# Top-k masks made beside the attention, and the memory's projections started with it, in a two-layer encoder on one core

## The chip, the cores and the metric

One Trainium2 chip, one NeuronCore of it. The time is device microseconds of one execution of the whole program. TensorE (PE in the rows, PEld its weight loads) multiplies, VectorE (DVE), ScalarE (ACT) and GpSimd (POOL) do elementwise work, SyncE (SP) issues the DMA transfers. Each engine takes its instructions in one fixed order and waits, at an instruction whose data are not there, with everything behind it. SBUF is the on-chip memory of 128 partitions, PSUM the eight banks into which TensorE writes. In the quoted rows sb is any SBUF buffer.

## The reference, cut to what matters

Two layers over x of 1024 tokens by 1024 features. The mixer of a layer has three branches: a gated convolution, DSA (each query attends to the 256 keys that a small indexer scores highest) and chunked band attention with a bias. Cross-attention into 256 memory tokens and a squared-ReLU MLP follow.

```python
def reference(x, mem, positions, w_in, ...):
    for l in range(DEPTH):                                   # DEPTH = 2
        mix = hybrid_mixer(x, positions, w_in[l], ...)
        x = layer_norm(ALPHA * x + mix, ...)
        cross = memory_cross_attention(x, mem, w_mq[l], w_mkv[l], w_mo[l])
        x = layer_norm(ALPHA * x + cross, ...)
        x = layer_norm(ALPHA * x + squared_relu_mlp(x, ...), ...)

def hybrid_mixer(...):
    proj = einsum(x, w_in)                # conv gates, dq dk dv, iq ik iw, cq ck cv
    y_conv = short_conv_mixer(...)
    y_dsa = dsa_attention(...)            # per query: top 256 of the indexer's scores,
                                          # softmax over them, times v; 6 heads of 64
    y_chk = chunk_band_attention(...)     # chunks of 64, band of 9 chunks; 6 heads of 64
    return einsum(concatenate([y_conv, y_dsa, y_chk]), w_out)

def memory_cross_attention(x, mem, w_q, w_kv, w_o):
    k, v = split(einsum(mem, w_kv), 2)    # these need no result of the mixer
    ...                                   # 4 heads of 256: softmax(q k) v, then w_o
```

## The kernel before, in words

**Arithmetic.** All of it is fp32, done on TensorE from two parts of each operand: a high part (a rounding cast) and a low part (what is left). A product is three matmuls, high x high (L340), low (L341, L342). An activation is split by a cast on ScalarE (L644) and a subtraction (L645, on VectorE or GpSimd). A weight is split when it is brought in: a load by SP's queue (L284), the high part's cast (L285), on ScalarE or, while `late` is set, on VectorE, and the low part on GpSimd (L286).

**What a layer does, in order.** First a front and a back run beside each other. The front computes the indexer's scores for query blocks 2 to 7 (128 queries each) and searches the 256th largest score of each query, bit by bit: 32 rounds in which blocks 7 and 6 are counted on ScalarE (L789) and blocks 5 to 2 on VectorE (L793). At the end of the search it makes for each of the six blocks a mask of 384 to 1024 columns, in 6 to 11 VectorE instructions (L845 to L860; the two large blocks also L828 to L843): it compares the scores with the threshold, counts what ties take, by a running sum (L856), and writes the mask (L860). The back computes the projections of the other branches, the convolution and its gate, and then the attention: the chunked one, 6 heads x 4 units of two query blocks, and the sparse one, 8 blocks x 2 groups of three heads.

**A unit of attention** multiplies scores into one of two banks for scores (L1054 chunked, L1184 sparse); VectorE adds bias or mask and takes the minimum, which empties the bank (L977); ScalarE takes the exponential (L983); GpSimd normalises (L994). Three units later in the pipeline TensorE transposes the rows (L1091, L1204), ScalarE and VectorE split them (L644, L645), and TensorE multiplies them with the values (L1105, L1213). Each head of the chunked part first prepares its queries (L1013 on VectorE, L1022 on GpSimd).

**The memory's projections** (`memory`) belong to the cross-attention, but need only the memory tokens: per layer 8 x 48 matmuls of 256 columns for keys and values, and 4 x 24 of 512 columns that multiply the values with the output weights. With them go 48 weights (32 of keys and values, 16 of the output), so 48 loads, casts and subtractions, and 16 blocks of products written to HBM (from L1373). They use one PSUM bank of their own, and serve as filler for TensorE beside the attention.

**What sets the order.** The pieces are Python generators that yield costs; `merge` always takes up the one whose sum of costs is least. `after(START, RATE, gen)` starts a generator at START and multiplies its costs by RATE. A scheduler then places the emitted instructions on each engine by priority and by its own model of durations; `shift` changes the priority of what a generator emits (FILL = 200 puts the memory's work back, 3000 the search). SBUF buffers come from one arena: a buffer that is freed is used again, and the new use waits for the old one.

Of the kernel before, what the change touches and what calls it, by code (L numbers as in the profile page):

```python
# [22 lines left out]
S = 1024  # L23
# [23 lines left out]
ROOMY = 8192  # L47
FILL = 200
TP = 2.5
START = 50  # L50
RATE = 2.0
EARLY = 0
STEP = 32
# [9 lines left out]
GROUPS = [(7, 6), (5, 4, 3, 2)]  # L63
# [192 lines left out]
class Weights:  # L256
# [17 lines left out]
    def _emit(self):  # L274
        k = self.k
        src, dims = self.specs[self.emitted]
        n = int(np.prod(dims))
        hl = k.sb.try_alloc(2 * n)
        if hl is None:
            return False  # L280
        st = self.stage[self.emitted % len(self.stage)].ap[:, :n]
        hi, lo = hl.r[:, :n], hl.r[:, n:]
        v = st if len(dims) == 1 else st.rearrange("p (a b) -> p a b", a=dims[0])
        k.nc.sync.dma_start(v, src)  # L284
        (k.nc.vector.tensor_copy if self.late else k.nc.scalar.copy)(hi, st)  # L285
        k.nc.gpsimd.tensor_tensor(lo, st, hi.bitcast(F32), op=ALU.subtract)  # L286
        self.units[self.emitted] = (hi, lo, hl)
        self.emitted += 1
        return True
# [21 lines left out]
class Kern:  # L311
# [449 lines left out]
    def topk(self, st):  # L761


        nc, sb = self.nc, self.sb


        groups = GROUPS
        junk, junk_a = sb.alloc(512), sb.alloc(512)
        tmp = [sb.alloc(S) for _ in range(2)]
        junkb = junk.ap.bitcast(BF16)  # L770
        junka = junk_a.ap.bitcast(BF16)
        col = sb.alloc(len(groups) * 32)
        state = []
# [7 lines left out]
        for bit in range(31, -1, -1):  # L781
            for g, blocks in enumerate(groups):
                cand, gone, cnt = state[g]
                ci, gi = cand.bitcast(I32), gone.bitcast(I32)
                for j, b in enumerate(blocks):
                    w = (b + 1) * P
                    x, c, n = st["score"][b].ap, cand[:, j : j + 1], cnt[:, j : j + 1]
# [26 lines left out]
                        op0=ALU.bitwise_xor, op1=ALU.bitwise_xor,  # L814
                    )
                yield TP * len(blocks) / 4
        for g, blocks in list(enumerate(groups))[::-1]:
            fl, cnt = state[g][0], state[g][2]
            for j, b in list(enumerate(blocks))[::-1]:
                w = (b + 1) * P  # L820
                sc = st["score"][b]
                tcol = fl[:, j : j + 1]
                eq, pre = (x.ap[:, :w] for x in tmp)
                if g == 0:


                    above, more = self.small(1), self.small(1)
                    nc.vector.tensor_scalar(  # L828
                        eq, sc.ap, tcol, None, op0=ALU.is_gt, op1=ALU.add,
                        accum_out=cnt[:, j : j + 1],  # L830
                    )
                    nc.vector.tensor_scalar(
                        eq, eq, -HIGH, HIGH, op0=ALU.mult, op1=ALU.add
                    )
                    nc.vector.tensor_tensor_reduce(
                        pre, sc.ap, eq, 1.0, HIGH, op0=ALU.add, op1=ALU.min,
                        accum_out=above,
                    )
                    nc.vector.tensor_scalar(
                        more.bitcast(I32), cnt[:, j : j + 1], float(TOPK), None,  # L840
                        op0=ALU.is_ge,
                    )
                    nc.vector.copy_predicated(tcol, more.bitcast(I32), above)  # L843

                nc.vector.tensor_scalar(  # L845
                    eq, sc.ap, tcol, BIG, op0=ALU.is_equal, op1=ALU.mult
                )
                nc.vector.tensor_scalar(
                    sc.ap, sc.ap, tcol, None, op0=ALU.is_le, op1=ALU.add,
                    accum_out=cnt[:, j : j + 1],  # L850
                )
                need = self.small(1)
                nc.vector.tensor_scalar(
                    need, cnt[:, j : j + 1], float(TOPK - w), BIG, op0=ALU.add, op1=ALU.mult
                )
                nc.vector.tensor_tensor_scan(pre, eq, eq, 0.0, op0=ALU.add, op1=ALU.max)  # L856
                nc.vector.scalar_tensor_tensor(
                    eq, pre, need, eq, op0=ALU.is_le, op1=ALU.mult
                )
                nc.vector.scalar_tensor_tensor(  # L860
                    sc.mask, sc.ap, BIG, eq, op0=ALU.mult, op1=ALU.subtract
                )
                sb.free(sc.high, self.w.late)
                yield 4.0
        for x in [junk, junk_a, col] + tmp:
            sb.free(x, self.w.late)

    def dsa_proj(self, l, xt, st):
        nc, sb = self.nc, self.sb
# [266 lines left out]
    def dsa_units(self, l, st):  # L1136


        nc, sb = self.nc, self.sb
# [33 lines left out]

        def scores(b, hg, heads):
            w = (b + 1) * P
            mask, qt = st["score"][b].mask, st["qt"][b]
            sm = self.small(3)
            for i in range(3):
# [763 lines left out]
    def build(self):  # L1942
        nc, sb = self.nc, self.sb
# [13 lines left out]
        for l in range(DEPTH):  # L1957
# [16 lines left out]
            def attention():  # L1974
                yield from self.pipeline(units())
                for x in ("dkT", "dv"):
                    sb.free(st.pop(x))

            def back():
                yield from self.dsa_proj(l, xt, st)  # L1980
                yield from self.chk_v(l, xt, st)
                for step in (
# [11 lines left out]
                self.ps.cls = dict(CLASSES)  # L1994
                self.w.reserve = RES
                self.w.late = LATE
                yield from self.merge(
                    attention(), self.after(START, RATE, self.shift(FILL, self.memory(l, st)))
                )

            self.ps.cls = {"S": (0, 1, 2, 3, 4, 5), "G": (6, 7)}
# [97 lines left out]
```

## Time and profile before

| what | value |
|---|---|
| median of the runs (three) | 3052.46 us (3051.95 to 3061.31) |
| profiled execution, its own time | 3054.18 us |
| its span | 3052.4 us |
| PE busy | 2894.9 us (95%), 14440 matmuls |
| DVE, ACT, POOL busy | 2239.0, 1527.2, 1317.6 us |
| mean granted TensorE clock | 0.973 |
| attention of layer 0, of layer 1 | about 284 to 580, 1809 to 2107 us of the span |

A row of a group reads: line, engine, operation, output and inputs with their shapes, how often; then busy time in us and the mean ns of one; then the idle time of that engine just ahead of these instructions and what ended it. A row of waits reads: waiting engine, buffer and line, the engine and line that it waits for, then us in all, how many, and the longest one. A row of time reads: start, duration, engine, line, operation.

### The profile page before, as it was taken

The page shows a single profiled execution, that of the slowest core. Times are in us where ns is not written, and L with a number is a line of the kernel's source. Part 1 is how long each engine was busy: PE and PEld are TensorE (multiplying, and loading weights), DVE is VectorE, ACT ScalarE, POOL GpSimd, SP SyncE. Part 2 cuts the span into 40 slices and gives each one's busy share as a digit, 9 for nine tenths or more (in the row PEclk, how much of TensorE's full clock was granted, in tenths as well). Part 3 has the DMA queues.
Part 4 walks back from the last instruction along what each step waited for, and adds up shares of the span by engine and source line. Part 5 has one row for each costly group of instructions (what it writes and reads, how often), then busy time and mean ns, then how long its engine had stood idle before and what let it go on. Part 6 is the DMA issues. An engine that isn't in the chain of part 4 may idle for free. (4 is left out here: it accounts for less than half of the span.)

```text
span 3052.4 us, 43458 instructions
## 1 busy us (share of the span) xinstructions
PE 2894.9 (95%) x14440; PEld 2452.0 (80%) x14440; DVE 2239.0 (73%) x4423; ACT 1527.2 (50%) x3074; POOL 1317.6 (43%) x1260
## 2 busy tenths in 40 slices
PE   8998799999999999999998987999999999999998
PEld 7886688878877788888787866887888777888886
DVE  5899978672478776777858998785725877667787
ACT  5676766513324455544456757665232344554442
POOL 4615566522335553232455154665223355532223
PEclk9999899999999999999999998999999999999999
DMA  3212133331325446755322121323312354466553
GB/s 125 55 43 57 50 102 113 116 114 39 105 101 175 165 154 223 247 186 189 123 71 55 39 65 41 116 93 125 114 52 101 110 174 162 152 249 227 182 180 115
DMA packets 261890, 374.14 MB, mean 123 GB/s; under 512 B 22560, under 2 KB 141344, under 8 KB 261664
## 3 DMA queue, kind: packets, MB, share of 16 engines
q1 hardware_dynamic: 261664, 371.35, 37.0%
q8 instruction: 114, 1.87, 0.2%
q14 instruction: 112, 0.92, 0.1%
HBM read 269.56 MB, written 95.42 MB: 120 GB/s over the span
## 5 line engine op out<-in xcount | busy, mean ns | idle before, releaser
L340 PE MATMUL banks<-sb,sb 128*128 128x512 f32 (+3 forms) x3776 | 1427.2, 379 | 31.8 <-DVE sb L645 11.7
L341 PE MATMUL banks<-sb,sb 128*128 128x512 f32 (+3 forms) x3776 | 1421.4, 377 | 6.0 <-POOL sb L286 5.9
L342 PE MATMUL banks<-sb,sb 128*128 128x512 f32 (+3 forms) x3776 | 1419.5, 377 | 6.5 <-POOL sb L645 6.5
L645 POOL TENSOR_TENSOR sb<-sb,sb 128x512 fp32r<-128x512 f32 (+1 forms) x428 | 588.1, 1386 | 946.1 <-ACT sb L644 834.9
L340 PEld LDWEIGHTS banks<-sb,sb 128*128 128x128 f32 x3776 | 717.0, 190 | 164.0 <-DVE sb L645 14.9
L342 PEld LDWEIGHTS banks<-sb,sb 128*128 128x128 f32 x3776 | 717.1, 190 | 132.0 <-POOL sb L645 7.3
L341 PEld LDWEIGHTS banks<-sb,sb 128*128 128x128 f32 x3776 | 717.6, 190 | 128.7 <-POOL sb L286 7.5
L644 ACT CAST sb<-sb 128x512 fp32r<-128x512 f32 (+1 forms) x788 | 452.5, 605 | 580.1 <-PE banks L341 135.1
L286 POOL TENSOR_TENSOR sb<-sb,sb 128x512 fp32r<-128x512 f32 (+2 forms) x288 | 376.3, 1319 | 512.0 <-ACT sb L285 403.7
L645 DVE TENSOR_TENSOR sb<-sb,sb 128x512 fp32r<-128x512 f32 x360 | 285.8, 821 | 41.6 <-ACT sb L644 41.3
L645 DVE TENSOR_TENSOR sb<-banks,sb 128x384 fp32r<-128x384 f32 (+2 forms) x324 | 187.8, 595 | 80.8 <-ACT sb L644 76.1
L644 ACT CAST sb<-banks 128x384 fp32r<-128x384 f32 (+2 forms) x324 | 160.0, 516 | 172.1 <-PE banks L1521 75.2
L793 DVE TENSOR_SCALAR_CACHE_REDUCE sb<-sb,sb 128x768 bf16<-128x768 f32 (+3 forms) x256 | 207.5, 811 | 4.9 <-POOL sb L749 2.3
L1685 DVE TENSOR_TENSOR sb<-sb,sb 128x512 f32<-128x512 f32 x160 | 158.4, 1025 | 56.9 <-ACT sb L1665 53.9
L1727 DVE TENSOR_TENSOR sb<-banks,sb 128x512 f32<-128x512 f32 x224 | 149.8, 683 | 45.9 <-PE banks L342 40.4
L983 ACT ACTIVATE sb<-sb,sb 128x640 f32<-128x640 f32 (+7 forms) x192 | 141.7, 739 | 77.5 <-DVE sb L977 73.2
L285 ACT CAST sb<-sb 128x512 fp32r<-128x512 f32 (+2 forms) x192 | 112.0, 599 | 125.9 <-PE banks L341 29.2
L994 POOL TENSOR_SCALAR sb<-sb,sb 128x128 f32<-128x128 f32 (+7 forms) x192 | 144.9, 770 | 66.6 <-DVE sb L992 60.6
L789 ACT ACTIVATE sb<-sb,sb 128x1024 bf16<-128x1024 f32 (+1 forms) x128 | 140.3, 1096 | 51.6 <-DVE sb L812 46.8
L1790 DVE TENSOR_TENSOR sb<-sb,sb 128x512 f32<-128x512 f32 x128 | 97.9, 767 | 70.5 <-DMA sb<-w_ff_dram 69.8
L1664 ACT ACTIVATE sb<-sb 128x512 f32<-128x512 f32 x128 | 80.7, 631 | 123.7 <-DVE sb L1727 123.5
L1582 DVE TENSOR_TENSOR sb<-sb,sb 128x512 f32<-128x512 f32 x96 | 91.6, 954 | 50.7 <-DMA h<-sb 30.7
(173 smaller groups left out, 3128.1 us busy)
## 6 DMA issues: line engine op xcount, KB each, us to landing
sb<-h SPq DMA_DIRECT2D x236, 256.0 KB, 3.1
h<-sb SPq DMA_DIRECT2D x224, 256.0 KB, 2.1
sb<-w_ff_dram SPq DMA_DIRECT2D x216, 256.0 KB, 3.1
sb<-w_ff_dram SPq DMA_DIRECT2D x64, 512.0 KB, 4.4
sb<-w_in_dram SPq DMA_DIRECT2D x64, 256.0 KB, 2.8
sb<-w_mkv_dram SPq DMA_DIRECT2D x64, 256.0 KB, 2.7
xs<-sb SPq DMA_DIRECT2D x24, 512.0 KB, 2.6
sb<-xs SPq DMA_DIRECT2D x24, 512.0 KB, 3.8
```

What stands on the lines that cost most here:

```text
L286: k.nc.gpsimd.tensor_tensor(lo, st, hi.bitcast(F32), op=ALU.subtract)
L340: mm(out, lh, rh, start=start, stop=False)
L341: mm(out, lh, rl, start=False, stop=False)
L342: mm(out, ll, rh, start=False, stop=stop)
L644: nc.scalar.copy(hi, src)
L645: eng.tensor_tensor(lo, src, hi.bitcast(F32), op=ALU.subtract)
L789: nc.scalar.activation(junka[:, :w], x, AF.Sign, bias=c, scale=-1.0, accum_out=n)
L793: nc.vector.tensor_scalar(junkb[:, :w], x, c, None, op0=ALU.is_ge, op1=ALU.add, accum_out=n)
L983: nc.scalar.activation(pt.ap, pt.ap, AF.Exp, bias=mn, scale=-1.0, accum_out=sm)
L994: nc.gpsimd.tensor_scalar(pt.ap, pt.ap, rc[:, i : i + 1], 0.0, op0=ALU.mult, op1=ALU.add)
L1685: nc.vector.tensor_tensor(z.ap, x, y, op=ALU.add if spec[1] == "+" else ALU.subtract)
L1727: nc.vector.tensor_tensor(r.ap, ps.ap, part[c, x].ap, op=ALU.add)
```

## The change

It has three parts. The masks are no longer made at the end of the search but by a generator of their own, `masks`, that runs beside the attention, a block per step; the scores of a sparse block run it on until the block's mask has been issued. Its two work buffers are taken per block, with the block's width, where the search held two of 1024 columns. The memory's projections start at cost 0 instead of 50 of the attention. And the high part of every weight is cast on ScalarE, while `late` is set too. What is computed, and with how many instructions, stays the same: only the 96 casts of the memory's weights (48 a layer) go from VectorE to ScalarE.

```diff
@@ -47,7 +47,7 @@
 ROOMY = 8192
 FILL = 200
 TP = 2.5
-START = 50
+START = 0
 RATE = 2.0
 EARLY = 0
 STEP = 32
@@ -282,7 +282,7 @@
         hi, lo = hl.r[:, :n], hl.r[:, n:]
         v = st if len(dims) == 1 else st.rearrange("p (a b) -> p a b", a=dims[0])
         k.nc.sync.dma_start(v, src)
-        (k.nc.vector.tensor_copy if self.late else k.nc.scalar.copy)(hi, st)
+        k.nc.scalar.copy(hi, st)
         k.nc.gpsimd.tensor_tensor(lo, st, hi.bitcast(F32), op=ALU.subtract)
         self.units[self.emitted] = (hi, lo, hl)
         self.emitted += 1
@@ -766,7 +766,6 @@
 
         groups = GROUPS
         junk, junk_a = sb.alloc(512), sb.alloc(512)
-        tmp = [sb.alloc(S) for _ in range(2)]
         junkb = junk.ap.bitcast(BF16)
         junka = junk_a.ap.bitcast(BF16)
         col = sb.alloc(len(groups) * 32)
@@ -814,13 +813,24 @@
                         op0=ALU.bitwise_xor, op1=ALU.bitwise_xor,
                     )
                 yield TP * len(blocks) / 4
-        for g, blocks in list(enumerate(groups))[::-1]:
+        sb.free(junk)
+        sb.free(junk_a)
+        st["found"] = state, col
+
+    def masks(self, st):
+
+        nc, sb = self.nc, self.sb
+        while "found" not in st:
+            yield 1.0
+        state, col = st.pop("found")
+        for g, blocks in list(enumerate(GROUPS))[::-1]:
             fl, cnt = state[g][0], state[g][2]
             for j, b in list(enumerate(blocks))[::-1]:
                 w = (b + 1) * P
                 sc = st["score"][b]
                 tcol = fl[:, j : j + 1]
-                eq, pre = (x.ap[:, :w] for x in tmp)
+                tmp = [sb.alloc(w) for _ in range(2)]
+                eq, pre = (x.ap for x in tmp)
                 if g == 0:
 
 
@@ -860,10 +870,11 @@
                 nc.vector.scalar_tensor_tensor(
                     sc.mask, sc.ap, BIG, eq, op0=ALU.mult, op1=ALU.subtract
                 )
-                sb.free(sc.high, self.w.late)
-                yield 4.0
-        for x in [junk, junk_a, col] + tmp:
-            sb.free(x, self.w.late)
+                for x in [sc.high] + tmp:
+                    sb.free(x, self.w.late)
+                st["masks"].add(b)
+                yield 7.5
+        sb.free(col, self.w.late)
 
     def dsa_proj(self, l, xt, st):
         nc, sb = self.nc, self.sb
@@ -1173,6 +1184,8 @@
 
         def scores(b, hg, heads):
             w = (b + 1) * P
+            while b not in st["masks"]:
+                next(st["mask steps"])
             mask, qt = st["score"][b].mask, st["qt"][b]
             sm = self.small(3)
             for i in range(3):
@@ -1994,8 +2007,16 @@
                 self.ps.cls = dict(CLASSES)
                 self.w.reserve = RES
                 self.w.late = LATE
+                st["masks"] = {0, 1}
+                st["mask steps"] = self.masks(st)
+
+                def mask_steps():
+                    for d in st["mask steps"]:
+                        yield 2.0 * d
+
                 yield from self.merge(
-                    attention(), self.after(START, RATE, self.shift(FILL, self.memory(l, st)))
+                    attention(), mask_steps(),
+                    self.after(START, RATE, self.shift(FILL, self.memory(l, st))),
                 )
 
             self.ps.cls = {"S": (0, 1, 2, 3, 4, 5), "G": (6, 7)}
```

What moves, at the three places that matter. The instructions of VectorE ahead of the first softmax step of layer 0, before (L856 to L860 are the mask of block 5, L828 and on the beginning of that of block 6, L1013 prepares a head's queries, L977 is the softmax step):

```order
L856 SCALAR_TENSOR_TENSOR sb_163<-sb_79 128x768
L1013 SCALAR_TENSOR_TENSOR sb_2723<-sb_1671,sb_2723 64x1024
L853 TENSOR_SCALAR sb_2510<-sb_1475 128x1
L857 SCALAR_TENSOR_TENSOR sb_79<-sb_163,sb_2510,sb_79 128x768
L860 SCALAR_TENSOR_TENSOR sb_281<-sb_280,sb_79 128x768
L828 TENSOR_SCALAR sb_79,sb_1475<-sb_282,sb_1475 128x896
L832 TENSOR_SCALAR sb_79<-sb_79 128x896
L839 TENSOR_SCALAR sb_2510<-sb_1475 128x1
L835 ISA sb_163,sb_2510<-sb_282,sb_79 128x896
L835 ISA sb_2510 128x1
L977 ISA sb_2706,sb_2510<-banks,sb_2628 128x128
```

and after (L799 and L811 are the search's last rounds, before L800 and L812; L954 is the convolution; L1024 was L1013, L988 was L977):

```order
L954 SCALAR_TENSOR_TENSOR sb_2512<-sb_149,sb_268,sb_2512 128x1022
L811 SCALAR_TENSOR_TENSOR sb_1475<-sb_1475 128x2
L799 TENSOR_SCALAR sb_1475<-sb_1475 128x1
L1024 SCALAR_TENSOR_TENSOR sb_2606<-sb_1671,sb_2606 64x1024
L799 TENSOR_SCALAR sb_1475<-sb_1475 128x1
L811 SCALAR_TENSOR_TENSOR sb_1475<-sb_1475 128x2
L1024 SCALAR_TENSOR_TENSOR sb_2774<-sb_1671,sb_2774 64x1024
L988 ISA sb_2657,sb_2654<-banks,sb_2604 128x128
L988 ISA sb_2654 128x1
L988 ISA sb_2762,sb_2654<-banks,sb_2604 128x256
```

Before, masks stand between the last of the search and the first softmax step; after, only the smallest one (384 columns) still does, some rows further up, and the others stand one instruction at a time between the softmax steps behind.

The same place on ScalarE, before (L983 is the exponential, L1021 prepares a head's keys):

```order
L983 ACT_TABLE_LOAD
L983 ACTIVATE sb_2706,sb_2510<-sb_2706,sb_2510 128x128
L983 ACTIVATE sb_2711,sb_2510<-sb_2711,sb_2510 128x256
L1021 CAST sb_2633<-sb_1937 64x512
L983 ACTIVATE sb_2716,sb_2510<-sb_2716,sb_2510 128x384
L983 ACTIVATE sb_2551,sb_2510<-sb_2551,sb_2510 128x512
L983 ACTIVATE sb_2743,sb_2510<-sb_2743,sb_2510 128x640
```

and after (L994 was L983; L285 is the cast of a weight's high part, L644 here that of the transposed memory tokens):

```order
L994 ACT_TABLE_LOAD
L994 ACTIVATE sb_2657,sb_2654<-sb_2657,sb_2654 128x128
L994 ACTIVATE sb_2762,sb_2654<-sb_2762,sb_2654 128x256
L285 CAST sb_2606<-sb_97 128x512
L994 ACTIVATE sb_2767,sb_2654<-sb_2767,sb_2654 128x384
L644 CAST sb_2667<-banks 128x4x128
L994 ACTIVATE sb_901,sb_2654<-sb_901,sb_2654 128x512
L285 CAST sb_2609<-sb_102 128x512
L994 ACTIVATE sb_930,sb_2654<-sb_930,sb_2654 128x640
```

The casts of the memory's weights now stand between the first exponentials.

TensorE in the sparse attention of the late blocks, before (L1184 scores, L1204 transposes, L1213 values; L340 to L342 are the memory's projections with the output weights):

```order
L1184 MATMUL banks<-sb_729,sb_4729 128x448 x2
L1213 MATMUL banks<-sb_3146,sb_620 128x384
L1204 MATMUL banks<-sb_67,sb_4690 128x128
L1204 MATMUL banks<-sb_67,sb_1082 128x128
L1204 MATMUL banks<-sb_67,sb_4757 128x128
L340 MATMUL banks<-sb_2658,sb_2674 128x512
L341 MATMUL banks<-sb_2658,sb_2674 128x512
L342 MATMUL banks<-sb_2658,sb_2674 128x512
L340 MATMUL banks<-sb_4838,sb_2674 128x512
L341 MATMUL banks<-sb_4838,sb_2674 128x512
L342 MATMUL banks<-sb_4838,sb_2674 128x512
```

and after (L1197, L1217 and L1226 are the same three lines):

```order
L1197 MATMUL banks<-sb_729,sb_4459 128x512 x4
L1226 MATMUL banks<-sb_5072,sb_620 128x384
L1217 MATMUL banks<-sb_67,sb_5052 128x128
L1217 MATMUL banks<-sb_67,sb_5079 128x128
L1217 MATMUL banks<-sb_67,sb_5101 128x128
L1226 MATMUL banks<-sb_5296,sb_620 128x384
L1226 MATMUL banks<-sb_4714,sb_620 128x384
L1226 MATMUL banks<-sb_4715,sb_620 128x384
L1226 MATMUL banks<-sb_2827,sb_620 128x384
```

Before, the memory's matmuls reach into the last blocks; after, all of them stand ahead of the values of sparse block 4, and the blocks behind it have none.

## The prediction

> **What bounds the kernel now.** I read the page first: which engine is nearly always busy, and where it is not.
>
> ```profile
> PE 2894.9 (95%) x14440; PEld 2452.0 (80%) x14440; DVE 2239.0 (73%) x4423; ACT 1527.2 (50%) x3074; POOL 1317.6 (43%) x1260
> ...
> PEclk9999899999999999999999998999999999999999
> ```
>
> TensorE works 95% of the span, so a microsecond is won only where PE idles or runs at a lower granted clock. Then the busy times by stretch, around the two attentions. The columns are: stretch, its length, busy us (and instructions) of PE, weight loads, DVE, ACT, POOL, then granted clock, DMA share, GB/s. The three rows of each layer are the attention's opening, its middle, and its tail (the sparse attention's blocks 4 to 7).
>
> ```profile
> 284.50:342.00 57.50, 31.40 (x130) 24.45 (x130) 53.27 (x99) 27.69 (x60) 41.76 (x32) 0.67 0.23 58
> 342.00:500.00 158.00, 146.93 (x1060) 134.12 (x1059) 130.30 (x375) 116.88 (x289) 97.38 (x124) 0.99 0.30 92
> 500.00:580.00 80.00, 74.86 (x470) 65.07 (x468) 61.32 (x146) 53.15 (x111) 46.90 (x41) 1.00 0.36 117
> 1809.00:1860.00 51.00, 28.88 (x109) 22.68 (x108) 48.54 (x98) 21.44 (x48) 34.56 (x33) 0.65 0.16 40
> 1860.00:2025.00 165.00, 152.40 (x1065) 138.37 (x1066) 131.63 (x379) 116.82 (x289) 104.40 (x127) 0.95 0.32 97
> 2025.00:2107.00 82.00, 80.91 (x513) 72.83 (x512) 62.16 (x146) 55.45 (x114) 37.42 (x35) 1.00 0.30 103
> ```
>
> The openings are holes: PE is busy 31.4 of 57.5 us, and at a clock of 0.67. At full clock that is 31.40 x 0.67 = 21.0 us of work; in layer 1, 28.88 x 0.65 = 18.8 us in 51.0. About 36 and 32 us are lost, while DVE is busy 93 to 95%. The waits of 284.5 to 342 say for whom PE waits, and DVE's order of time says what DVE does before its first softmax step (L977):
>
> ```profile
> PE banks L1054 <- DVE sb L977: 20.1, 3, 8.1
> PE banks L1054 <- DVE sb L1013: 4.7, 1, 4.7
> ...
> 283.37 1.69 DVE L857 SCALAR_TENSOR_TENSOR sb<-sb,sb,sb 128x640 f32<-128x640 f32 x1
> 304.45 0.28 DVE L977 CUSTOM_DVE_ANT_0 sb<-banks,sb 128x128 f32<-128x128 f32 x1
> ```
>
> The chunk scores (L1054) wait for banks that L977 empties, and L977 stands behind masks. The masks' main groups on DVE, 267 to 342:
>
> ```profile
> L856 DVE TENSOR_TENSOR_SCAN sb<-sb 128x384 f32<-128x384 f32 (+5 forms) x6 | 9.9, 1650 | 0.0
> L857 DVE SCALAR_TENSOR_TENSOR sb<-sb,sb,sb 128x384 f32<-128x384 f32 (+5 forms) x6 | 8.0, 1327 | 0.1
> L860 DVE SCALAR_TENSOR_TENSOR sb<-sb,sb 128x384 bf16<-128x384 f32 (+5 forms) x6 | 7.4, 1240 | 0.1
> L848 DVE TENSOR_SCALAR_CACHE_REDUCE sb<-sb,sb 128x384 f32<-128x384 f32 (+5 forms) x6 | 5.7, 946 | 0.1
> L845 DVE TENSOR_SCALAR sb<-sb,sb 128x384 f32<-128x384 f32 (+5 forms) x6 | 4.6, 767 | 0.1
> L835 DVE CUSTOM_DVE_ANT_0 sb<-sb,sb 128x896 f32<-128x896 f32 (+1 forms) x2 | 3.5, 1754 | 0.0
> ```
>
> These are 39.1 us a layer for six widths, 4224 columns together.
>
> **The change, part by part.** *The masks.* None is removed. In the new order the first one (384 columns, 9% of the work, 3.5 us) still stands in the search; about 36 us come later, single steps between softmax steps. The chunked attention does not need them, the sparse one does, block by block, and the last is done near the end of the chunked part: nobody waits for it early. What the opening keeps is the wait for L1013 (4.7 us) and a few us until the pipeline of units is filled, at half clock. I take 8 us, bounds 4.7 and 12.
>
> *The memory's projections from the start.* Each layer has 384 matmuls of 256 columns and 96 of 512 that need no attention. By the order all of them now stand before block 4 of the sparse attention. So they fill the opening and are missing in the tail. What they are worth in the tail of layer 0, by PE's groups in 500 to 580 (L340 to L342 are the memory's there):
>
> ```profile
> L1213 PE MATMUL banks<-sb,sb 128*128 128x384 f32 x99 | 29.5, 367 | 2.9 <-DVE sb L645 1.4 <-ACT sb L644 1.1
> L1204 PE MATMUL banks<-sb,sb 128*128 128x128 f32 x150 | 23.8, 272 | 0.0
> L1184 PE MATMUL banks<-sb,sb 128*128 128x448 f32 (+2 forms) x56 | 17.7, 395 | 1.0 <-DVE sb L977 1.0
> L340 PE MATMUL banks<-sb,sb 128*128 128x256 f32 (+1 forms) x51 | 17.1, 336 | 0.0
> L342 PE MATMUL banks<-sb,sb 128*128 128x256 f32 (+1 forms) x51 | 16.6, 325 | 0.0
> L341 PE MATMUL banks<-sb,sb 128*128 128x256 f32 (+1 forms) x51 | 16.2, 318 | 0.6 <-POOL sb L286 0.6
> ```
>
> The rows overlap each other; the memory's share is 49.9 of 120.9, and of PE's 74.86 us that is 30.9. They go to the front.
>
> *The high parts on ScalarE.* 48 casts a layer leave DVE. Their busy time by stretch (DVE, then ACT), the price of one on ACT, and how DVE waited for their loads:
>
> ```profile
> 284.50:500.00 215.50, 19.75 (x33) 1.22 (x2) 0.90 0.28 83
> 500.00:580.00 80.00, 9.41 (x16) 0.62 (x1) 1.00 0.36 117
> 2025.00:2107.00 82.00, 8.22 (x12) 0.00 (x0) 1.00 0.30 103
> ...
> L285 ACT CAST sb<-sb x192: 429/620/682, 4.8 to 2312.8; 128x512 fp32r<-128x512 f32 x160, 128x296 fp32r<-128x296 f32 x16, 128x384 fp32r<-128x384 f32 x16
>   DMA sb<-w_mkv_dram: 9.6, 13
> ...
> DMA to landing us min/median/max: 2.5/2.7/4.3
> ```
>
> DVE loses 29 us a layer; ACT gains 48 x 0.62 = 30. What the projections issue beside this moves with them: 48 loads and 16 writes of products a layer on SP's queue, a subtraction (L286) on POOL behind each cast. DMA engines are busy 0.23 to 0.36 of the attention, so I cost their earlier start at nothing; were that cover gone, rival 4 prices it.
>
> *The sum for layer 0.* Front work on PE: 21.0 + 146.93 x 0.99 + 30.9 = 197. At what rate? The middle has stretches without the memory's matmuls (342 to 380, 1860 to 1910) and with them:
>
> ```profile
> 342.00:380.00 38.00, 34.48 (x237) 29.50 (x236) 35.21 (x111) 36.47 (x87) 21.45 (x30) 1.00 0.27 66
> 380.00:500.00 120.00, 112.45 (x825) 104.61 (x824) 95.09 (x265) 80.42 (x203) 75.93 (x95) 0.99 0.31 100
> 1860.00:1910.00 50.00, 44.39 (x301) 38.62 (x301) 42.69 (x135) 43.87 (x106) 27.32 (x38) 0.94 0.19 52
> 1920.00:2025.00 105.00, 101.60 (x733) 94.66 (x733) 82.56 (x227) 66.81 (x167) 72.99 (x83) 0.97 0.38 119
> ```
>
> That is 78.9 of 88 us (0.90) without and 214.1 of 225 (0.95) with them. The new front is filled throughout, but it also carries the masks on DVE and the casts on ACT, so I take 0.93, bounds 0.90 and 0.95: 197 / 0.93 = 212 us. Do the others fit in? DVE: 53.3 + 130.3 - 19.8 plus some 7 us of masks that lay before 284.5 is 171; ACT: 27.7 + 116.9 + 46 x 0.62 plus 8 copies of the tail (0.59 each) is 178. Both are below 212.
>
> The tail, without filler: PE has 74.86 - 30.9 = 44 us left, DVE 61.32 - 9.41 = 51.9, ACT about 48. DVE is the longest. In the unfilled stretches above DVE was busy 77.9 of 88 us (0.89): 51.9 / 0.89 = 58 us, bounds 0.85 and 0.95 (61 and 55).
>
> Layer 0: 8 + 212 + 58 = 278 us against 295.5 (284.5 to 580), 17.5 less. Layer 1: front 18.8 + 152.40 x 0.95 + 30.9 = 194.5, over 0.93 is 209; tail (62.16 - 8.22) / 0.89 = 61; 8 + 209 + 61 = 278 against 298, 20 less. Together 37.5. The profiled execution took 3054.2 us, 1.7 above the median of the runs: 3054.2 - 37.5 - 1.7 = **3015 us**. Its own bounds: front 0.90 costs 14, 0.95 gives 9; the tail 5 or 8; the opening 8 or 7. Not all at once: 2998 to 3035.
>
> *A rule against it.* A mask step reads two SBUF operands, as L857 does, and POOL is at work all through the attention. L857 on 640 columns took 1.69 us (above) just ahead of a stretch in which POOL is busy 41.8 of 57.5 us, on 1024 columns only 1.28 while POOL stood idle 13.4 us:
>
> ```profile
> 328.81 1.28 DVE L857 SCALAR_TENSOR_TENSOR sb<-sb,sb,sb 128x1024 f32<-128x1024 f32 x1
> 334.23 1.28 POOL L1022 TENSOR_TENSOR sb<-sb,sb 64x512 fp32r<-64x512 f32 x1 [13.40 <-ACT sb L1021]
> ```
>
> The Trainium skill (SBUF — State Buffer, section SBUF: two separate sides) says that VectorE and GpSimd take a shared pair of ports as an exclusive lock for a whole instruction, the other blocked; the two rows agree. What it makes of the time is the third rival.
>
> **The rivals.**
>
> 1. *All of the hole is won.* Front at 0.95, tail at 0.95, opening 4.7: 4.7 + 207 + 55 = 267 and 4.7 + 205 + 57 = 267, so 28.5 + 31 less: 2993 us. For it: 0.97 in 1920 to 2025. Against: ACT and DVE are both above 80% then.
> 2. *The masks stall the softmax where they now stand.* Every step on DVE delays the L977 behind it, and two banks hold scores. If half of the 36 us shows on PE in each layer, 36 of the 37.5 us are gone: 3051, no change. Against: DVE has 41 us free in the front.
> 3. *POOL and masks exclude each other.* POOL in the front: 41.8 + 97.4 + 16 x 1.3 (its part of the moved units) = 160; with 36 of masks 196, under 212. So it decides nothing by itself; if the same 0.93 applied to a chain of 196 plus the three L1013 (2.1 us each in the hole), 203 / 0.93 = 218, six us a layer: 3027.
> 4. *Slower: ACT waits for the memory's loads.* A cast on ACT whose load is late holds every exponential (L983) and high part (L644) behind it. ACT has 34 us of slack a layer, and the gain is 19 more: 48 casts may wait 1.1 us each before the kernel loses. With half a landing time (1.35 us) each, ACT needs 178 + 65 = 243 us, 31 more than the front: 12 a layer lost, 3077 us. Against: DVE waited only 9.6 us for w_mkv in all, 0.15 us for each of the 64 loads. For: the loads are wanted twice as fast at the start.
> 5. *The change does not do what it says.* The order shows that it does, but for the first mask.
>
> **How the numbers follow.** A measurement of this kernel tells about 0.3%, 9 us, from no change. Chances: the forecast 0.54 and rival 3 0.09, both faster; a front near 0.88 with a slow tail, 3035 to 3043, 0.05, faster; rival 1 0.15, faster; rival 2 0.10, of it 0.08 within 0.3% and 0.02 slower; rival 4 0.07, slower. Together: faster 0.83, same 0.08, slower 0.09. The range 2989 to 3044 leaves out rival 4, most of rival 2 and a little of rival 1 below.
>
> **What would show it.** Right: the waits of PE L1054 (L1065 in the changed lines) for the softmax step fall from 20 us to a few in each layer; the granted clock of the openings rises from 0.67 and 0.65 to above 0.9; memory matmuls stand within 20 us of the first scores; the attention of layer 0 ends near 562 instead of 580; the tail runs with PE at about 0.75 to 0.8 and DVE at about 0.9. DVE's total falls by some 55 us, ACT's rises by some 60. Wrong: ACT idle before L285 for a DMA by tens of us (rival 4); L1065 still waiting for DVE in the whole chunked part (rival 2); longer POOL instructions there (rival 3); or a tail of over 65 us, where the lost filler takes back what the opening gave.

## The result, and the profile after

The changed kernel took 3025.95 us in the median (3022.03 to 3031.39, four runs); the kernel before, beside it, 3053.51 us. The ratio is 0.9906 (0.9882 to 0.9929): about 28 us faster. A later set, with more runs of the kernel before, gave 0.9909 (0.9892 to 0.9925). The forecast was 3015 us with a range of 2989 to 3044. The time lies in the range, but about a quarter of the forecast gain is missing.

The page of the changed kernel, the rows that answer to those shown of before:

```profile
PE 2892.3 (96%) x14440; PEld 2443.2 (81%) x14440; DVE 2169.2 (72%) x4327; ACT 1572.6 (52%) x3170; POOL 1310.0 (43%) x1260
...
PEclk9999999999999999999999999999999999999999
```

Both dips of the granted clock are gone. The same stretches of the two attentions, layer 1's moved by the 13 us by which its attention now begins earlier (first score at 1792.9 instead of 1805.8):

```profile
284.50:342.00 57.50, 50.23 (x308) 43.28 (x307) 35.15 (x97) 42.30 (x91) 42.26 (x43) 0.91 0.45 117
342.00:500.00 158.00, 141.80 (x963) 126.58 (x962) 128.04 (x329) 121.78 (x291) 110.75 (x122) 0.96 0.33 102
500.00:580.00 80.00, 74.35 (x425) 62.35 (x424) 64.14 (x166) 64.85 (x138) 31.91 (x34) 0.96 0.18 62
1796.00:1847.00 51.00, 43.07 (x283) 39.35 (x284) 37.09 (x101) 38.10 (x86) 38.80 (x38) 0.90 0.38 102
```

The openings hold 308 matmuls instead of 130, and 283 instead of 109. But the middle holds fewer than before, 963 instead of 1060, and its clock is 0.96 instead of 0.99. So some of what the opening won is given back behind it. The last value product of the attention comes 290.4 us after its first score in layer 0 (298.3 before), and 289.1 in layer 1 (301.5): 20.3 us of the profiled execution's 30. Another 7 us lie in the output projection and the cross-attention right behind, up to the first transposes of the MLP (L1521): from first score to there 565.5 and 564.7 us became 554.6 and 548.4. All the rest of the program gave 2.8 us.

TensorE's longest waits in the first opening, now:

```profile
PE banks L1336 <- DMA sb<-mem_dram: 3.0, 1, 3.0
PE banks L340 <- ACT sb L1386: 1.6, 1, 1.6
PE banks L1065 <- DVE sb L1024: 0.8, 1, 0.8
...
PE banks L1065 <- DVE sb L988: 0.4, 2, 0.2
```

The wait of the scores for the softmax step (20.1 us before) is down to 0.4; in layer 1's opening it fell from 12.1 to 3.9. There TensorE had also waited 9.2 us for GpSimd's normalisation (the longest 6.8, while GpSimd still had convolution steps and splits ahead of it); in the changed kernel's opening it is gone too. The new ones are short: the load of the memory tokens, and copies out of the memory's single bank.

### The profile page after: what moved, and what is told of

Its sections match the earlier page's. It is cut to its first block, busy times and chain, and to the rows that moved or that the text cites. A ratio compares the mean times of both kernels' runs of the same rounds, so it can differ in the third digit from the quotient of the medians.

```text
span 3022.4 us, 43528 instructions
## 1 busy us (share of the span) xinstructions
PE 2892.3 (96%) x14440; PEld 2443.2 (81%) x14440; DVE 2169.2 (72%) x4327; ACT 1572.6 (52%) x3170; POOL 1310.0 (43%) x1260
## 5 line engine op out<-in xcount | busy, mean ns | idle before, releaser
L340 PE MATMUL banks<-sb,sb 128*128 128x512 f32 (+3 forms) x3776 | 1425.9, 379 | 31.5 <-ACT sb L644 15.2
L342 PE MATMUL banks<-sb,sb 128*128 128x512 f32 (+3 forms) x3776 | 1414.9, 376 | 3.0 <-POOL sb L645 2.9
L645 POOL TENSOR_TENSOR sb<-sb,sb 128x512 fp32r<-128x512 f32 (+1 forms) x428 | 587.7, 1385 | 918.1 <-ACT sb L644 784.3
L340 PEld LDWEIGHTS banks<-sb,sb 128*128 128x128 f32 x3776 | 716.1, 190 | 164.1 <-ACT sb L644 17.4
L342 PEld LDWEIGHTS banks<-sb,sb 128*128 128x128 f32 x3776 | 714.8, 189 | 128.5 <-POOL sb L645 4.5
L644 ACT CAST sb<-sb 128x512 fp32r<-128x512 f32 (+1 forms) x788 | 452.3, 605 | 534.1 <-DVE sb L1595 96.7
L286 POOL TENSOR_TENSOR sb<-sb,sb 128x512 fp32r<-128x512 f32 (+2 forms) x288 | 386.1, 1357 | 490.2 <-ACT sb L285 448.3
L645 DVE TENSOR_TENSOR sb<-sb,sb 128x512 fp32r<-128x512 f32 x360 | 287.9, 827 | 44.6 <-ACT sb L644 43.8
L285 ACT CAST sb<-sb 128x512 fp32r<-128x512 f32 (+2 forms) x288 | 168.9, 605 | 153.8 <-PE banks L342 22.4
L644 ACT CAST sb<-banks 128x384 fp32r<-128x384 f32 (+2 forms) x324 | 158.6, 516 | 169.9 <-PE banks L1534 106.6
L645 DVE TENSOR_TENSOR sb<-banks,sb 128x384 fp32r<-128x384 f32 (+2 forms) x324 | 186.0, 594 | 76.6 <-ACT sb L644 74.2
L1698 DVE TENSOR_TENSOR sb<-sb,sb 128x512 f32<-128x512 f32 x160 | 155.5, 1005 | 65.6 <-ACT sb L1678 65.5
L994 ACT ACTIVATE sb<-sb,sb 128x640 f32<-128x640 f32 (+7 forms) x192 | 141.3, 738 | 29.4 <-DVE sb L988 24.3
L1803 DVE TENSOR_TENSOR sb<-sb,sb 128x512 f32<-128x512 f32 x128 | 98.6, 771 | 73.1 <-DMA sb<-w_ff_dram 73.0
L1595 DVE TENSOR_TENSOR sb<-sb,sb 128x512 f32<-128x512 f32 x96 | 85.6, 892 | 51.6 <-DMA h<-sb 28.8
```

The source lines that it names most:

```text
L285: k.nc.scalar.copy(hi, st)
L340: mm(out, lh, rh, start=start, stop=False)
L342: mm(out, ll, rh, start=False, stop=stop)
L644: nc.scalar.copy(hi, src)
L645: eng.tensor_tensor(lo, src, hi.bitcast(F32), op=ALU.subtract)
L994: nc.scalar.activation(pt.ap, pt.ap, AF.Exp, bias=mn, scale=-1.0, accum_out=sm)
```

## The experiments

All ratios are against the kernel before, run on the same chip beside the others; the sets ran on three chips, so kernels of different sets are compared by their ratios. Theory A, with the result known: VectorE paces the chunked part; what wins is that its masks no longer stand in one block ahead of the first softmax steps, and what is missing of the gain is what the masks cost where they stand now.

**One part at a time.** Four kernels take the change apart. The first has only the masks moved (START and the casts as before):

```diff
-START = 0
+START = 50
-        k.nc.scalar.copy(hi, st)
+        (k.nc.vector.tensor_copy if self.late else k.nc.scalar.copy)(hi, st)
```

> Only the masks move; the memory's projections start at 50 as before, their casts stay on VectorE. Theory A (VectorE sets the pace of the opening, and spreading the masks is what closes the hole): the 20 us waits of the chunk scores for the softmax step go, but the unfilled chunked part stays at VectorE's pace (about 119 us of its work in the 135 us up to the memory's start, 0.88; at 0.93 it takes 128), so 7 to 12 us a layer: 3030 to 3040 us. Rival B (the filler closes the hole, not the masks' move): within 5 us of before, 3048 to 3056 us.

The second keeps the early start and ScalarE's casts and runs all the mask steps at the search's end (it differs from the kernel before in the buffers, too: it has the change's smaller ones):

```diff
                 yield from self.shift(3000, self.topk(st))
+                st["masks"] = {0, 1}
+                st["mask steps"] = self.masks(st)
+                yield from self.shift(3000, st["mask steps"])
...
-                    attention(), mask_steps(),
+                    attention(),
```

> The masks stay at the search's end (with the new, smaller buffers), the memory starts at 0 with its casts on ScalarE. Theory A: the softmax steps still stand behind some 36 us of masks, PE can do only the memory matmuls that stand between the first scores, and the tail has lost its filler: 3040 to 3055 us. Rival B (filler is what counts): as good as the whole change, 3020 to 3032 us.

The third is the kernel before with `k.nc.scalar.copy(hi, st)` in L285 and nothing else:

> Only the high parts' casts go to ScalarE. They lie in the filled middle and in the tail, where PE is busy 93% and VectorE is not the bound. Theory A: within 0.3% of before, 3045 to 3057 us. Rival C (the casts on VectorE delay the memory's matmuls): 5 us or more a layer gained, under 3044 us. Rival D (ScalarE waits for loads): over 3060 us.

The fourth is the changed kernel with the casts back on VectorE:

> The whole change but for the casts, which stay on VectorE. Theory A (VectorE is the tightest engine of the front, where masks and casts now meet): the 30 us of casts a layer come back to it, and the front takes 5 to 10 us more a layer than with the whole change: 3033 to 3046 us. Rival D (the casts on ScalarE cost what they save): 3022 to 3031 us, as the whole change.

A fifth is the changed kernel with START = 50:

> The whole change but for the early start: the memory's projections begin at 50 again. Masks alone gave a ratio of 0.9920, the casts alone 0.9978, the whole change 0.9906. Theory A (the early start carries filler from the tail to the front and is worth nothing in sum): the two add up, 0.988 to 0.991. Rival B (part of the gain needs the filler in the opening): 0.992 or more.

And the change itself was measured once more:

> The changed kernel itself once more, beside more runs of the kernel before, since the other kernels are compared with its ratio of 0.9906 (0.9882 to 0.9929). Theory A (the early start is worth nothing or costs a little, for masks and casts without it gave 0.9892): 0.989 to 0.992. Rival B (the early start does win): under 0.989.

| masks moved | start at 0 | casts on ScalarE | ratio (95% interval) |
|---|---|---|---|
| no | no | yes | 0.9978 (0.9968 to 0.9987) |
| no | yes | yes | 0.9980 (0.9969 to 0.9991) |
| yes | no | no | 0.9920 (0.9903 to 0.9937) |
| yes | yes | no | 0.9928 (0.9913 to 0.9942) |
| yes | no | yes | 0.9892 (0.9876 to 0.9908) |
| yes | yes | yes | 0.9909 (0.9892 to 0.9925) |

Read in pairs. The masks' move is worth 0.0080 alone, 0.0086 beside ScalarE's casts, 0.0071 beside these and the early start: 22 to 26 us of 3055, so nearly the whole gain. In the third pair both kernels have the small buffers, so the gain does not come from these. ScalarE's casts are worth 0.0022, 0.0028 and 0.0019 (the last within the noise of its two ratios): 6 to 9 us for some 60 us of work taken off VectorE. The early start is worth nothing in any pair: +0.0002, +0.0008, +0.0017, each within the intervals. Theory A held in the first, third and fifth run. In the fourth the casts back on VectorE cost 6 us where I had priced 5 to 10 a layer, so by its ratio that kernel ended between the two theories (its 3037.1 us lie in theory A's range only because the kernel before took 3058 us on that chip). In the second the sum is theory A's, but the layers are not: in its profiled execution (3046.1 us, one of its fastest) layer 0 became 12.5 us shorter than before from first score to L1521 (553.0) and layer 1 11.5 us longer (576.2). Its waits show what stays when the masks do not move:

```profile
PE banks L1065 <- DVE sb L988: 18.7, 10, 12.3
...
PE banks L1065 <- DVE sb L988: 15.5, 10, 9.2
```

The first row is layer 0, the second layer 1. The scores still wait for the softmax step, and the attention from the first score to the last value product took 301.5 and 302.1 us, no less than before (298.3 and 301.5). So the filler made up for nothing there. The layers differ behind the attention, up to L1521: 251.5 us with 1259 matmuls in layer 0, 274.1 us with 1328 in layer 1 (before 267.2 with 1299, and 263.2 with 1292). In layer 0 more matmuls had already been placed among the attention's last; what put them there is not settled.

**Why the early start is worth nothing.** Here are the chunked part (first to last chunk score) and the sparse part (first to last value product) of both layers, of the changed kernel:

```profile
286.80:438.00 151.20, 131.59 (x856) 115.75 (x857) 118.56 (x295) 109.86 (x243) 112.48 (x109) 0.94 0.41 115
459.60:577.20 117.60, 110.89 (x679) 95.40 (x678) 91.38 (x244) 95.43 (x213) 51.79 (x60) 0.96 0.20 66
1792.90:1938.10 145.20, 123.12 (x834) 110.30 (x832) 116.14 (x293) 107.09 (x240) 107.78 (x105) 0.95 0.39 110
1962.70:2082.00 119.30, 113.15 (x692) 96.06 (x693) 92.79 (x237) 93.60 (x208) 57.50 (x64) 0.99 0.21 71
```

and of the kernel with masks and casts but without the early start:

```profile
286.90:410.00 123.10, 102.53 (x629) 88.31 (x630) 103.91 (x284) 92.89 (x212) 76.97 (x88) 0.89 0.25 67
430.40:573.00 142.60, 136.24 (x898) 120.40 (x897) 96.72 (x249) 109.39 (x242) 79.88 (x82) 1.00 0.32 102
1795.20:1914.60 119.40, 95.94 (x618) 82.09 (x617) 100.85 (x281) 88.65 (x207) 74.11 (x88) 0.94 0.25 72
1939.50:2075.90 136.40, 130.47 (x856) 116.85 (x854) 95.02 (x239) 107.24 (x234) 77.91 (x80) 0.99 0.33 109
```

The early start puts 227 more matmuls into layer 0's chunked part, which takes 28.1 us longer: 0.124 us for each. It takes 219 out of the sparse part, which takes 25.0 us less: 0.114 each. Layer 1 reads the same way, 216 more in 25.8 us, and 164 fewer in 17.1. That is near what a matmul costs where TensorE never idles (20.00 us busy for 157 of them in 480 to 500 of the kernel before, 0.127 each). These 157 have other widths, so by width: of those moved into layer 0's chunked part some 199 have 256 columns and 48 have 512, and back to back these start every 0.12 and 0.23 us, so together some 33 us; 28.1 is most of it. The unfilled chunked part showed PE busy 102.5 of 123.1 us, and still the filler did not go into the 20 idle us: with it 19.6 are idle. The row alone does not say why; the engines of a unit wait for each other in turn, and a filler matmul ahead of a score in TensorE's order makes that score late. What is shown is the price, not this reason. The whole layer gives the same answer: with the early start the attention is 4.3 and 8.4 us longer (290.4 and 289.1 us against 286.1 and 280.7) and holds 12 and 34 more matmuls; the stretch behind it, up to L1521, has as many fewer and is 6.3 and 10.8 us shorter.

**What the masks cost where they now stand.** The changed kernel without the running sum and the step behind it:

```diff
-                nc.vector.tensor_tensor_scan(pre, eq, eq, 0.0, op0=ALU.add, op1=ALU.max)
-                nc.vector.scalar_tensor_tensor(
-                    eq, pre, need, eq, op0=ALU.is_le, op1=ALU.mult
-                )
```

> The whole change, but the masks leave out the handling of ties (the running sum and the step behind it), so about 18 of the 36 us of mask work a layer are not done. Theory A (the masks, now between the softmax steps, slow the front through VectorE): 4 to 9 us a layer faster than the whole change, ratio 0.985 to 0.988. Rival E (VectorE has room there, as the prediction's sum has it): within 2 us a layer of the whole change, 0.9895 to 0.9915.

It took a ratio of 0.9833 (0.9817 to 0.9849), more than theory A had asked for: 0.0076 below the changed kernel, 23 us or 11.6 a layer, for some 18 us of VectorE's work a layer (0.6 us for each; by the two intervals 0.4 to 0.8). The parts that shrank (chunked, sparse, by layer):

```profile
291.50:431.90 140.40, 122.44 (x834) 110.08 (x833) 100.79 (x281) 106.93 (x240) 104.98 (x109) 0.94 0.42 120
455.60:568.90 113.30, 105.58 (x670) 90.94 (x669) 88.56 (x237) 94.03 (x208) 51.08 (x60) 1.00 0.20 64
1783.50:1921.20 137.70, 121.79 (x833) 109.62 (x833) 102.26 (x282) 105.02 (x235) 98.78 (x103) 0.95 0.40 115
```

The chunked part, in which the masks stand, is 10.8 and 7.5 us shorter; the sparse part of layer 0 4.3. So VectorE, busy only 118.6 of 151.2 us in the changed kernel's chunked part, has no free room for these steps: a microsecond of them costs about 0.6. Whether the other half of the mask work costs as much was not tried. One place where this is seen, 400 to 440 of the changed kernel, and the same stretch before:

```profile
400.00:420.00 20.00, 18.27 (x117) 16.36 (x118) 19.62 (x45) 12.87 (x29) 12.90 (x10) 0.91 0.52 160
420.00:440.00 20.00, 16.71 (x117) 14.32 (x115) 19.18 (x45) 12.99 (x32) 14.91 (x16) 0.99 0.28 85
```

```profile
400.00:420.00 20.00, 19.17 (x162) 19.15 (x163) 14.18 (x39) 8.73 (x21) 17.20 (x18) 1.00 0.35 107
420.00:440.00 20.00, 19.89 (x150) 18.59 (x150) 14.14 (x50) 16.74 (x50) 11.37 (x18) 1.00 0.38 126
```

VectorE is busy 38.8 of 40 us there, with the masks of the two large blocks, and TensorE gets 234 matmuls through instead of 312. The two stretches do not hold the same work, so this is an example and no measure of the masks' cost.

**Moving the masks about.** Three times as far apart (the costs of `mask_steps` times 6 instead of 2), then this with RATE = 3:

> The whole change, with the masks' steps three times as far apart (costs times 6 instead of 2): they are done after 45, 84, 108, 113 and 120 of a layer's 144 softmax steps instead of 23, 35, 40, 57 and 64. Theory A (VectorE is over 95% busy in 400 to 440 because masks crowd there): 2 to 6 us a layer faster than the whole change, ratio 0.986 to 0.989. Rival E: no difference, 0.990 to 0.992.

> As with the masks spread, and the memory's projections at rate 3 instead of 2, from 0 as in the change: by the order their matmuls now reach block 6 of the sparse attention, so neither the opening nor the tail is without filler. Theory A (the tail pays for what the front was given, since without filler its PE waits for the splits): 3 to 8 us a layer faster than with the masks spread alone, ratio 0.982 to 0.986. Rival F (the filler is worth the same wherever it stands): as with the masks spread alone, within 0.001.

0.9946 (0.9931 to 0.9962) and 0.9920 (0.9904 to 0.9935). The first went against both theories: it is 11 us slower than the change. Its chunked and sparse part of layer 0:

```profile
288.90:425.40 136.50, 126.05 (x850) 113.72 (x851) 87.22 (x257) 107.56 (x241) 97.68 (x108) 0.94 0.43 119
448.70:587.70 139.00, 118.10 (x663) 94.83 (x661) 114.05 (x282) 93.95 (x208) 56.61 (x62) 0.91 0.18 59
```

The chunked part is indeed 14.7 us shorter than the changed kernel's. But the masks of the large blocks now stand in the sparse part, whose late blocks have no filler: VectorE's busy time there goes from 91.4 to 114.1 us, and the part takes 139.0 us instead of 117.6. RATE = 3 wins 0.0026 on that, 8 us or 4 a layer, as theory A had it, though from a worse kernel than the change; the intervals leave this gain just clear of noise.

> The whole change with the memory's projections at rate 3 instead of 2 and the masks' steps at 1.5 instead of 2 (with 2 the buffers do not fit): the masks are done at nearly the same softmax steps (63 of 144 instead of 64), the memory's matmuls stand in the order from the first head to sparse block 6. Theory A (filler is worth the same in the front as in the tail as long as both are short of it, so that spreading wins a little): 0.986 to 0.989. Rival F (worth the same wherever it stands): 0.9895 to 0.9915.

> As with the masks moved and the casts on ScalarE, memory from 50 (ratio 0.9892), and the masks' steps half as far apart: done after 5, 23, 33, 43 and 51 softmax steps of a layer instead of 25, 33, 53, 65 and 84. Masks three times as far apart had cost 0.004. Theory A (masks belong where the softmax steps need VectorE least; late ones meet the sparse part, which needs it most): 0.986 to 0.989. Rival H (early masks crowd the opening again, and the chunk scores wait): 0.991 or more.

Rate 3 with the masks nearly where they were (the costs of their steps times 1.5): 0.9933 (0.9920 to 0.9947), 7 us slower than the change; neither theory had that. Masks half as far apart, without the early start: 0.9955 (0.9942 to 0.9967), 19 us slower than the same kernel with the change's spacing; rival H was right. The chunked part of layer 0 in that last kernel:

```profile
288.00:418.30 130.30, 100.38 (x596) 87.31 (x597) 112.93 (x297) 91.48 (x209) 77.47 (x85) 0.86 0.21 57
```

and its longest waits of layer 0's attention:

```profile
PE banks L1065 <- DVE sb L988: 11.0, 7, 6.1
PE banks L1102 <- POOL sb L1005: 8.3, 6, 2.3
```

The chunk scores wait for the softmax step again (11.0 us, 7.0 with the change's spacing), and the chunked part takes 130.3 us instead of 123.1. The longest wait, 6.1 us, is not only a matter of crowding: right ahead of it VectorE stood still for 3.6 us at a mask step (L855), until a convolution step on GpSimd (L970) was done. So the spacing of the change lies between two losses: earlier masks hold up the opening, later ones the sparse part. Why rate 3 alone loses is not settled; its chunked parts take 147.0 and 158.3 us.

**Another engine for a part of the masks.** The last step on GpSimd:

```diff
-                nc.vector.scalar_tensor_tensor(
-                    sc.mask, sc.ap, BIG, eq, op0=ALU.mult, op1=ALU.subtract
-                )
+                nc.gpsimd.tensor_scalar(
+                    pre, sc.ap, BIG, 0.0, op0=ALU.mult, op1=ALU.add
+                )
+                nc.gpsimd.tensor_tensor(sc.mask, pre, eq, op=ALU.subtract)
```

> The whole change, with the last step of every mask on GpSimd as two instructions instead of one on VectorE: some 7 us of VectorE's 36 us of mask work a layer go, GpSimd gets some 20 us. Leaving out 18 us a layer had given 0.0073 against the whole change (0.9833 against 0.9906), 0.6 us for each us. Theory A (VectorE's time between the softmax steps is what the masks cost): 4 us a layer faster than the whole change, ratio 0.987 to 0.9895. Rival G (GpSimd, 70% busy in the chunked part, becomes late with the normalisation and the low parts): 0.991 or more.

0.9911 (0.9897 to 0.9924), no difference to the change. It is rival G's outcome; GpSimd's busy time in layer 0's chunked part rose from 112.5 to 121.9 us, and VectorE's fell by 3.2, less than half of the 7.1 us that the step had taken in that layer. That GpSimd's lateness ate the gain is not shown; nor is what made VectorE's other work there longer.

## Why the prediction was right, and where its sum was off

**The bound.** Right. The holes at the openings were the masks' doing: moving them alone gives a ratio of 0.9920, and PE's wait of 20.1 us for the softmax step in layer 0's opening is down to 2.1 in that kernel.

**The sum.** To read it by its own steps I cut the attention near where the prediction did, at the 40th value product of the sparse part (the count at 500 and 2025 before; at 511 and 2016.5 of the changed kernel it is 38, and the 40th starts at 513.1 and 2017.0, so the fronts are short by 2.1 and 0.5 us and the tails long by as much). The columns are those of the stretches above:

```profile
284.50:511.00 226.50, 203.04 (x1336) 179.94 (x1335) 170.90 (x450) 171.99 (x398) 156.33 (x169) 0.95 0.37 108
511.00:573.00 62.00, 56.35 (x332) 46.60 (x331) 51.45 (x133) 53.62 (x115) 26.20 (x26) 0.97 0.08 29
1796.00:2016.50 220.50, 194.96 (x1305) 173.35 (x1306) 168.46 (x453) 166.65 (x390) 147.00 (x162) 0.95 0.36 107
2016.50:2082.00 65.50, 61.55 (x357) 50.35 (x356) 55.80 (x129) 51.61 (x110) 34.27 (x32) 1.00 0.13 43
```

| term | forecast | measured |
|---|---|---|
| layer 0, opening and front | 8 + 212 | 226.5 |
| layer 0, tail | 58 | 62 |
| layer 1, opening and front | 8 + 209 | 220.5 |
| layer 1, tail | 61 | 65.5 |
| both attentions, against before | -37.5 | -19 |
| elsewhere | 0 | -11 (profiled execution) |

(The 20.3 us told above are counted from the first score, which in layer 0 itself came 2.4 us earlier, to the last value product; the table has the prediction's cuts.) Two steps of the sum were mis-sized.

- *The rate of the front, 0.93 of full speed.* The amount of work came out near: 203.04 us busy at a clock of 0.95 is 193 us at full clock, against 197, though the 30.9 us for the memory in it were too many (next point). The rate was too high: 193 of 226.5 us is 0.85 with the opening in it, where 197 of 220 made 0.90. I had taken the rate from stretches in which the clock was 0.97 to 0.99 and VectorE had no masks to do, and asked only whether VectorE's 171 us fit into 212. Its busy time came out as forecast (170.90). But the fit of the sums says nothing about waits. TensorE idled 23.5 us in this front and 27.2 in layer 1's. Of that 4.0 and 10.2 us were waits for the softmax step, which stands behind mask steps; most of the rest is spread over waits for splits (L645, L644), for copies and for a load. The run without ties shows that masks cost time there; which part of the shortfall is theirs is not shown.
- *The tail.* VectorE was forecast to set it at 0.89 busy; it was busy 51.45 of 62.00 us and 55.80 of 65.50, 0.83 and 0.85, with PE at 0.91 and 0.94 where I had expected 0.75 to 0.8. The step that failed is the memory's share of PE's time there, 30.9 us. I had split PE's busy time by the sums of the groups' rows. But without the memory's matmuls the sparse part's own keep PE busy 56.35 us in layer 0, not 44; the overlapping rows don't split in proportion. The trace of the kernel before could have told: in its 500 to 580 the time in which any matmul but L340 to L342 was at work is 55.6 us, which leaves 19 of the 74.86 to the memory. By that PE, not VectorE, is the longest engine of the tail.

A third term was missing: the 11 us elsewhere. Part of it lies behind the attention, where PE no longer waits (before, then after, each from the last value product to 45 us past the MLP's first transposes):

```profile
587.00:900.00 313.00, 308.71 (x1532) 260.76 (x1531) 166.58 (x334) 82.69 (x187) 92.01 (x89) 0.99 0.27 92
```

```profile
577.00:887.00 310.00, 310.00 (x1549) 261.95 (x1548) 160.70 (x331) 81.40 (x184) 93.71 (x92) 1.00 0.28 96
```

I did not test what it comes from. That it brought the total nearer to the forecast is luck: in the attentions alone only half of the forecast gain was found.

**The memory's early start.** The mechanism was right, the order and the trace show the filler in the opening and none in the tail; but the prediction let it fill a hole that the masks' move had already closed. Counted alone, it moved 25 to 28 us in layer 0 from one part to the other and won nothing.

**ScalarE's casts.** VectorE's busy time fell by 69.8 us (55 forecast) and ScalarE's rose by 45.4 (60 forecast). Rival 4 is out: ScalarE waited little for loads ahead of L285 between 284 and 500:

```profile
ACT sb L285 <- DMA sb<-w_mkv_dram: 6.2, 6, 1.9
```

That is 6.2 us in one layer (in 1796 to 2016 of layer 1 8.3, for both weights), not the 65 that the rival asked for. (The DMA share that the prediction read as 0.23 to 0.36 is 0.16 in one of its rows, 1809 to 1860; nothing hangs on it.)

**The other rivals.** Rival 1 (2993 us) would have needed the front and the tail at 0.95. Rival 2, the masks stalling the softmax steps where they now stand, was given 0.10 as a case of its own; it is a part of the truth, as the run without ties shows: 0.6 us for each us left out is even more than the half that this rival took. Its conclusion, no gain, was wrong: the time fell by 28 us. Rival 3 would show in longer instructions. The three mask groups with the most time, in layer 0, were L856 9.9, L857 8.0 and L860 7.4 us before; in the changed kernel:

```profile
L866 DVE TENSOR_TENSOR_SCAN sb<-sb 128x384 f32<-128x384 f32 (+5 forms) x6 | 11.6, 1929 | 0.0
L870 DVE SCALAR_TENSOR_TENSOR sb<-sb,sb 128x384 bf16<-128x384 f32 (+5 forms) x6 | 7.1, 1190 | 0.1
L867 DVE SCALAR_TENSOR_TENSOR sb<-sb,sb,sb 128x384 f32<-128x384 f32 (+5 forms) x6 | 6.6, 1094 | 0.0
```

25.3 us both times, while GpSimd was busy 112.5 of 151.2 us beside them. So rival 3 has nothing in the sum of the masks' times. The sign that the prediction named, longer GpSimd instructions, is small: the mean of L286 went from 1382 ns in 284.5 to 500 of the kernel before to 1436 ns in 284.5 to 511, that of the normalisation of 640 columns from 828 to 856, some 4 us of GpSimd's time together. The Trainium skill (SBUF — State Buffer, section SBUF: two separate sides) has the lock that the prediction quoted; these sums neither show it at work nor exclude it, since GpSimd was busy in the opening before, too.

**Of the signs named ahead,** these came: the fallen wait, the clock (0.91 and 0.90), memory matmuls near the first scores. These did not: layer 0's attention ending near 562 (the output projection begins at 573), and the tail with PE at 0.75 to 0.8 and VectorE at 0.9. One sign of being wrong was touched: layer 1's tail took 65.5 us where over 65 was named. It did not take back what the opening gave; before, that tail had taken 82.

**The best version** is the change without its early start: 0.9892 (0.9876 to 0.9908) against 0.9909 (0.9892 to 0.9925). The intervals overlap, so it is as fast or a few us faster, with one edit less. The kernel without tie handling is faster than both, but computes less.

## What to carry to other kernels

A hole in TensorE's work is closed by removing what makes its queue wait. Once that is done, work pulled forward into the hole only changes place: here the moved matmuls cost most of their full time in a stretch that showed 17% idle. Idle shares of engines that wait for each other need not be room. And before work is put between the steps of such a chain, ask what a microsecond of it costs there (0.6 here, for the steps that were left out), not whether the engine's busy times add up to less than the stretch.

## What was not expected of the hardware

The granted clock is part of a stage's price, even when no long hole is left: in the changed kernel's front it was 0.95 in the mean, with PE's single waits of at most 3 to 4 us, and 0.90 to 0.91 in stretches like the opening. In the sparse part, with PE busy 96% in the kernel without the early start, it was 0.99 to 1.00. It does not simply follow the busy share of the same stretch: in the changed kernel it was 0.91 in 400 to 420, with PE busy 18.27 of 20 us, and 0.99 in 420 to 440, with 16.71.
